# Short convolution's blocks in pairs by seven products ahead of linear attention, other filler in their place, and the down stages' h kept in float32

## The chip, the cores and the metric

One core of a Trainium2 chip runs the whole program in one launch. The metric is the device time of that launch in microseconds, the median of the runs. The engines are TensorE (PE: matrix products and transposes), VectorE (DVE), ScalarE (ACT), GpSimd (POOL) and SyncE (SP, which issues most transfers). Each works through its own instructions in the order in which they stand in the program, and waits at one until what it needs is there.

## The reference

One layer of an encoder is applied to two groups of tokens with the same weights: x_sample with 512 tokens (stream S in the kernel) and x_prompt with 256 (stream P), 1024 features each, in float32.

```python
x = LN(a*x + 0.5*swiglu(x, ffn1_gu, ffn1_down))        # 2816 hidden
x = LN(a*x + parallel_mixer(x))
x = LN(a*x + memory_cross_attention(x, mem, ...))      # 256 memory rows, 4 heads of 256
x = LN(a*x + 0.5*swiglu(x, ffn2_gu, ffn2_down))

# parallel_mixer: one projection x @ w_in gives all of these
h, gb, gc, q, k, v, g, lr_f, lr_b, m_conv, m_gla = split(x @ w_in)
y_conv = (gb * short_conv(gc * h, conv_w)) @ w_conv_out     # width 512, three taps along the tokens
o      = gla_forward(q, k, v, lr_f) + gla_backward(...)     # 4 heads, chunks of 64 tokens
y_gla  = (rms(o) * norm_g * silu(g)) @ w_gla_out
merged = (sigmoid(m_conv) * y_conv + sigmoid(m_gla) * y_gla) @ w_out
```

Linear attention runs over chunks of 64 tokens: within a chunk products of q and k decayed by a running sum of log gates, between chunks a state of 64 x 128 per head and direction.

## The kernel before

**Products.** A float32 operand is split into a rounded part (fp32r, high) and the rest (low): `split` (L86) copies on ACT to the high part and subtracts on DVE for the low one. A product is then three matmuls, high x high, low x high, high x low (`mm3`, L105 to L108; tile names xh, xl for tokens and wh, wl for weights). `load_w` (L90) loads a block of weights of 128 x 1024, 512 KB, and splits it; of the loaded block (raw) there are three buffers, of the split ones five.

**Seven products.** `seven` (L410) computes two blocks of 128 output columns over all 768 tokens as a 2 x 2 product by seven products instead of eight; tokens come in halves of 384. `products(b)` (L489) issues P1, P5, P6, P3, P7, P2, P4, each 12 matmuls with 384 columns (lines L473, tiles px, py, pz); `snap` copies a sum to SBUF on ACT and `added` adds on DVE. The sums of weights that a pair needs are made by `weights_of` while the pair before runs (`behind`).

**Feed-forward.** `front1` and `front2` do the first blocks (`plain_block`, L593), then `block` (L540) takes the rest of the 22 blocks by seven products. `gated` (L560) splits every block's h into hq and stores the pair of halves in `hspill` (768 KB, or 384), and stores sums of h in `sspill`. `down_seven` (L221) multiplies h with the down weights, again by seven products (tiles dn): it loads split h as ao from `hspill` (`direct`) or float32 sums as sr from `sspill`, which it splits (`summed`); four ao buffers, three sr buffers. `down_last` does the blocks that stay in SBUF.

**Mixer.** `mixer` (L666) makes values, queries, keys and low-rank gates, then ten pairs by seven products: two for silu(g) (stored in `silud`) and eight for the two merge gates (stored in `sigd`). Then comes linear attention, head by head: `gate(h)` (L817) multiplies the low-rank gates (z on PE) and works on DVE and ACT through la, the scans c, dd, f, kin, qin, qst; `inner` (L863) transposes kin (kt), multiplies kin and qin (at), and keys with values (kv), and carries the state st on DVE; `outputs` (L911) makes o. DVE and ACT need long for that, so PE gets other work between: `fill(ns)` (L198) takes units from the generator at the head of `pending` until their stated durations reach ns. Here that is `conv()` (L945): twelve blocks of 128 output columns (h, gc and gb of the four column blocks), each for both streams; u = gc * h and the three taps follow on DVE, and `uc` stays in SBUF. How much is filled is set by GFILL:

```python
        pending.append(conv())
        g = gate(0)
        fill(GFILL[0])
        for h in range(4):
            st = inner(h, *g)
            nxt = gate(h + 1) if h < 3 else None
            fill(GFILL[1])
            outputs(h, g[3], st)
            if h % 2:
                rms_scale(h // 2)
            fill(GFILL[2])
        drain()
```

`rms_scale` (L927) squares o on ACT, sums on DVE and takes a reciprocal root in thirteen small steps; the scaling of o (acc by rms, L1008) and the output projections follow (`branch`, L1010: tiles pt, results t and sig).

**Cross attention.** `tok_out` (L1046) makes the mixer's last product and adds; after the norm `to_T` (L183) transposes the tokens (lt) into xh, xl. Stream S and stream P each have a `Cross`: `keys_values` (L1097) is a generator with eight units for keys K and eight for values V. Those of S fill around the transposes (FILL[0], FILL[1]; `drain` takes the rest ahead of `attend`, L1186), those of P likewise in P's own stage.

**Order.** The text above is program order. A layer that records the program moves instructions ahead of others that it predicts to wait, on each engine; the places quoted below are from the order that comes of it.

Of the kernel before, what the change touches and what calls it, by code (L numbers as in the profile page):

```python
# [15 lines left out]
NK = 8  # L16
# [10 lines left out]
LO_K = (5, 7)  # L27
LO_V = (1, 3)
# [4 lines left out]
GFILL = (16000, 10000, 8000)  # L33
FILL = (14000, 14000, 8000, 14000)
# [24 lines left out]
def _encoder(ctx, tc, nc, io, out, dbg):  # L59
# [161 lines left out]
    def down_seven(n, wdn, pairs, keep, dr, sd, order6, load_acc, ahead):  # L221
# [3 lines left out]
        with tc.tile_pool(name=f"seven{n}", bufs=1, reuse_waits="tile") as pool:  # L225
            V = nc.vector
            nd = len(pairs)
            raw = [pool.tile([128, 1024], F32, name=nid("raw7")) for _ in range(2)]
# [11 lines left out]
            def loaded(q, d):  # L240
                turn[0] += 1
                if turn[0] % 5 in (4, 0):
                    r = raw[turn[0] % 5 // 4]
# [11 lines left out]
            def ring():  # L255
                return pool.tile([128, 2, 2, HT], F32R, tag="ao", bufs=4, name=nid("ao"))

            def direct(t, par, d):

                if d == 0:  # L260
                    return [keep[2 * kp + par][:, t] for kp in pairs[d]]
                a = ring()
                kp = pairs[d][0]
                last_load[0] = nc.sync.dma_start(a[:].bitcast(F32), dr[:, t, par, kp:kp + 2])
                return [a[:, k] for k in range(2)]

            def summed(s, d):
                r = pool.tile([128, 2, HT], F32, tag="sr", bufs=3, name=nid("sr"))
                kp = pairs[d][0]
                last_load[0] = nc.sync.dma_start(r[:], sd[:, s, kp:kp + 2])  # L270
# [44 lines left out]
            for d in own[:-1]:  # L315
                P1(d)
                if d == 0:
                    load_acc(0, 0)
                P2(d)
            P2(own[-1])  # L320
# [89 lines left out]
    def seven(X, pool, more, tt, snap_t, sum_t):  # L410
# [78 lines left out]
        def products(b):  # L489
# [4 lines left out]
            p1 = snap(x, "p1")  # L494
            y = psum(nid("py"))[:, :HT]
# [16 lines left out]
    def ffn_fast(n, i, front, order6, src, groups, last):  # L512

        wgu, wdn = io[f"ffn{n}_gu"], io[f"ffn{n}_dn"]
        dr = dp.tile([128, 2, 2, NFB // 2, 2, HT], F32, name=f"hspill{n}")
        sd = dp.tile([128, 4, NFB // 2, HT], F32, name=f"sspill{n}")
# [21 lines left out]
        keep = {}  # L538

        def block(j, b):  # L540
            g1, x, up1, up2 = products(b)
# [18 lines left out]
        def gated(j, h32):  # L560
# [32 lines left out]
        def plain_block(j, b, before=None):  # L593
# [15 lines left out]
            gated(j, h32)  # L609
# [46 lines left out]
        down_seven(n, wdn, groups, keep, dr, sd, order6, load_acc, ahead)  # L656
# [6 lines left out]
        right.close()  # L663


    def mixer(i):  # L666
# [7 lines left out]
        mo = ExitStack()  # L674
# [20 lines left out]
        def low_rank(s):  # L695
# [7 lines left out]
            t = fx.tile([128, TT], F32, tag="big", bufs=3, name=nid("lrt"))[:32, :s.T]  # L703
# [54 lines left out]
        def big(nm):  # L758
            return fx.tile([128, TT], F32, tag="big", bufs=3, name=nid(nm))

        for k in range(4):
            a = []
            for q in (k, k + 4):
                x = big("x0")
                nc.vector.tensor_tensor(x[:], xh["all"][:, q, :].bitcast(F32), xl["all"][:, q, :].bitcast(F32),
# [7 lines left out]
        pairs = [(w_g(2 * c), w_g(2 * c + 1), AF.Silu, silud, 2 * c) for c in range(2)]  # L773
        pairs += [(wm[16 + 2 * c], wm[17 + 2 * c], AF.Sigmoid, sigd, 2 * c) for c in range(8)]
# [3 lines left out]
        for n, (_, _, fn, dst, c) in enumerate(pairs):  # L778
            g1, x, u1, u2 = products(ws)
            first, second = big("first"), big("second")  # L780
            for half, (g, u) in enumerate(((g1, u1), (x, u2))):
                hc = slice(half * HT, (half + 1) * HT)
                nc.scalar.activation(first[:, hc], g, fn)
                nc.scalar.activation(second[:, hc], u, fn, scale=-1.0)
            nc.scalar.dma_start(dst[:, c, :], first[:])
            nc.scalar.dma_start(dst[:, c + 1, :], second[:])
# [6 lines left out]
        mop = mo.enter_context(tc.tile_pool(name="mixo", bufs=1, reuse_waits="tile", side="right"))  # L793
# [14 lines left out]
        cw = gp.tile([128, 4, 3], F32, name="cw")  # L808
        nc.sync.dma_start(cw[:], io["conv_w"])
# [129 lines left out]


        uc = []
        co = {"S": slice(0, TS), "P": slice(TS + 1, TT + 1)}
        uo = {"S": slice(1, TS + 1), "P": slice(TS + 2, TT + 2)}

        def conv():  # L945
            for b in range(4):
                u = gp.tile([128, TT + 3], F32, tag="u", bufs=1, name=nid("u"))
                for z in (0, TS + 1, TT + 2):
                    nc.gpsimd.memset(u[:, z:z + 1], 0.0)
                w = load_w(wm[4 + b])  # L950
                for s in STREAMS:
                    ps = proj_T(w, s)
                    nc.scalar.activation(u[:, uo[s.name]], ps, AF.Copy)
                    yield s.T * 10.2
                w = load_w(wm[8 + b])
                for s in STREAMS:
                    ps = proj_T(w, s)
# [483 lines left out]
```

## Time and profile before

| | us |
|---|---|
| median of three runs | 1776.19 (1775.16 to 1776.35) |
| the profiled execution: its time | 1774.76 |
| its span, first to last instruction | 1773.0 |
| PE without work in the span | 17.6 |
| linear attention, first gate product to last output (724.8 to 861.4) | 136.6 |
| all DMA | 267.26 MB, mean 151 GB/s |

The profile's page gives for each engine its busy time and share of the span, for each line the groups of instructions that cost most, and the chain of work that ended last, followed back from the last instruction. Other views list what an engine waited for, one stretch in order of time, and busy time by stretches. Times in them are microseconds from the start of the span, mean durations nanoseconds. A matmul's busy time overlaps that of the next one; what a matmul costs is read from the chain, where starts follow each other.

### The profile page before, as it was taken

To read this page: it belongs to the slowest core of one execution; us is meant where nothing else is said; L and a number is where in the kernel's file an instruction comes from. 1 tells how busy PE (TensorE), PEld (TensorE's weight loads), DVE (VectorE), ACT (ScalarE), POOL (GpSimd) and SP (SyncE) were. 2 spreads that over 40 slices of the span, in tenths; PEclk is the share of its full clock that TensorE was granted. 3 is DMA by queue.
4 is the path that set the end of the run, shared out by engine and by line. 5 is a ranking of instruction groups with operands and counts; after the bars stand their busy time and mean duration, and the time that the engine had idled before them with its cause. 6 is when DMAs were issued, how large, how long until landed. Compare 5 with 4: busy or idle time off the path is not lost.

```text
span 1773.0 us, 25183 instructions
## 1 busy us (share of the span) xinstructions
PE 1755.4 (99%) x9758; PEld 1613.7 (91%) x9758; DVE 1258.9 (71%) x2157; ACT 767.1 (43%) x1297; POOL 26.0 (1%) x60
## 2 busy tenths in 40 slices
PE   9999999999999999999999999999999999999998
PEld 9999999878889999888888988899899999997886
DVE  8777777487569555579775964596697777765956
ACT  6444444243235544655232253344354444443521
POOL 0000000000100000000000000000000000000002
PEclk9999999999999999999999999999999999999999
DMA  5434333598433333311363262255424444328961
GB/s 199 152 125 156 128 137 114 195 324 300 170 108 95 125 125 125 118 36 53 122 220 131 83 191 72 84 197 162 152 85 147 139 144 140 132 88 319 346 220 72
DMA packets 100535, 267.26 MB, mean 151 GB/s; under 512 B 10016, under 2 KB 23584, under 8 KB 100416
## 3 DMA queue, kind: packets, MB, share of 16 engines
q1 hardware_dynamic: 92352, 248.88, 40.9%
q10 hardware_dynamic: 8064, 16.78, 2.6%
q8 instruction: 76, 1.25, 0.3%
q14 instruction: 43, 0.35, 0.1%
HBM read 212.15 MB, written 53.48 MB: 150 GB/s over the span
## 4 chain that ended last, share of the span: by engine, by line
PE 94%; DVE 3%; DMA 1%; ACT 1%; issue 0%; SPq 0%; DVEq 0%; ACTq 0%
PE px L473 23%; PE py L473 11%; PE dn L283 11%; PE pz L473 6%; PE pt L106 6%; PE pt L107 6%; PE pt L108 6%; PE to L108 2%; PE to L106 2%; PE to L107 2%; PE dn L107 2%; PE dn L106 2%; PE dn L108 2%; PE pp L473 1%; PE lt L191 1%; DMA raw<-in_ffn_dn_dram 1%
## 5 line engine op out<-in xcount | busy, mean ns | idle before, releaser
L88 DVE TENSOR_TENSOR wl<-raw,wh 128x512 fp32r<-128x512 f32 (+2 forms) x309 | 289.4, 939 | 167.9 <-ACT wh L87 167.2
L87 ACT ACTIVATE wh<-raw 128x512 fp32r<-128x512 f32 (+2 forms) x309 | 255.9, 831 | 333.8 <-PE pt L107 83.5
L283 PE MATMUL dn<-wh,ao 128*128 128x512 f32 x600 | 185.8, 390 | 1.7 <-DMA ao<-hspill 1.2
L106 PE MATMUL pt<-xh,wh 128*128 128x512 f32 (+2 forms) x512 | 173.1, 338 | 0.0
L107 PE MATMUL pt<-xl,wh 128*128 128x512 f32 (+2 forms) x512 | 172.4, 337 | 0.0
L108 PE MATMUL pt<-xh,wl 128*128 128x512 f32 (+2 forms) x512 | 172.0, 336 | 0.0
L283 PEld LDWEIGHTS dn<-wh,ao 128*128 128x128 f32 x600 | 112.5, 188 | 25.8 <-DMA ao<-hspill 1.6
L87 ACT ACTIVATE wh<-tt 128x512 fp32r<-128x512 f32 x156 | 95.3, 625 | 78.4 <-PE px L473 36.7
L283 PE MATMUL dn<-wl,ao 128*128 128x512 f32 x300 | 117.4, 391 | 3.1 <-DVE wl L88 3.0
L88 DVE TENSOR_TENSOR wl<-tt,wh 128x512 fp32r<-128x512 f32 x156 | 105.3, 687 | 1.9 <-ACT wh L87 0.2
L106 PEld LDWEIGHTS pt<-xh,wh 128*128 128x128 f32 x512 | 97.0, 190 | 9.8 <-issue 0.5
L108 PEld LDWEIGHTS pt<-xh,wl 128*128 128x128 f32 x512 | 96.9, 189 | 9.0
L107 PEld LDWEIGHTS pt<-xl,wh 128*128 128x128 f32 x512 | 97.0, 190 | 8.7 <-issue 0.2
L473 PE MATMUL px<-xh,wl 128*128 128x384 f32 x232 | 77.5, 334 | 0.0
L473 PE MATMUL px<-xh,wh 128*128 128x384 f32 x232 | 77.5, 334 | 0.0
L473 PE MATMUL px<-xl,wh 128*128 128x384 f32 x232 | 77.5, 334 | 0.0
L546 DVE SCALAR_TENSOR_TENSOR h<-sil,sum 128x384 f32<-128x384 f32 x78 | 43.4, 557 | 46.4 <-ACT sil L545 46.4
L545 ACT ACTIVATE sil<-sum 128x384 f32<-128x384 f32 x39 | 20.5, 525 | 118.8 <-DVE sum L485 118.8
L283 PEld LDWEIGHTS dn<-wl,ao 128*128 128x128 f32 x300 | 56.3, 188 | 17.0 <-DVE wl L88 5.5
L106 PE MATMUL dn<-wh,hr 128*128 128x512 f32 (+1 forms) x150 | 57.7, 385 | 0.0
L107 PE MATMUL dn<-wl,hr 128*128 128x512 f32 (+1 forms) x150 | 57.5, 383 | 0.0
L108 PE MATMUL dn<-wh,hr 128*128 128x512 f32 (+1 forms) x150 | 57.4, 383 | 0.0
(372 smaller groups left out, 4678.9 us busy)
## 6 DMA issues: line engine op xcount, KB each, us to landing
raw<-in_ffn_gu_dram SPq DMA_DIRECT2D x84, 512.0 KB, 3.5
raw<-in_ffn_dn_dram SPq DMA_DIRECT2D x64, 512.0 KB, 5.7
hspill<-hq SPq DMA_DIRECT2D x24, 768.0 KB, 3.7
raw<-in_w_mix_dram SPq DMA_DIRECT2D x32, 512.0 KB, 3.5
ao<-hspill SPq DMA_DIRECT2D x18, 768.0 KB, 5.8
sr<-sspill SPq DMA_DIRECT2D x32, 384.0 KB, 5.3
sspill<-hs SPq DMA_DIRECT2D x56, 192.0 KB, 2.3
hr<-hspill SPq DMA_DIRECT2D x24, 384.0 KB, 6.8
```

Of the source, the lines that this page charges most:

```text
L87: nc.scalar.activation(hi, src, AF.Copy)
L88: (lo_eng or nc.vector).tensor_tensor(lo, src, hi.bitcast(F32), op=ALU.subtract)
L106: nc.tensor.matmul(o, lh, rh, start=start, stop=False)
L107: nc.tensor.matmul(o, lh, rl, start=False, stop=False)
L108: nc.tensor.matmul(o, ll, rh, start=False, stop=stop)
L191: nc.tensor.transpose(ps[:, j * 128:(j + 1) * 128], A[:, c:c + 128], ident[:])
L283: nc.tensor.matmul(ps[t][:], l, r[:, o], start=start and k == 0 and m == 0, stop=stop and k == 1 and m == 2, skip_group_check=True)
L473: nc.tensor.matmul(ps, l[:, c], r[:, k, :], start=st and n == 0, stop=sp_ and n == 2, skip_group_check=True)
L545: nc.scalar.activation(sil[:], g, AF.Silu)
L546: ins = nc.vector.scalar_tensor_tensor(h32[:, half * HT:(half + 1) * HT], sil[:], -0.5, u, ALU.mult, ALU.mult)
```

## The change

**Convolution by pairs.** The generator conv() goes. Six pairs are added to the ten of the mixer: four with h and gc of one column block (finish u and the taps, result stored in the DRAM tile `ucd`), two with gb of two column blocks (load ucd, multiply, store). After linear attention `branch` loads ucd and splits it into xh, xl.

**Other filler.** In its place linear attention is filled with the keys of both memories (16 units) and half the values of S (4 units). The memories are loaded and split ahead of it; finished blocks go to DRAM tiles `kvdS`, `kvdP` on ACT's queue (`kept`), and `fetch` and `take` bring them back in cross attention. GFILL and FILL get smaller numbers; S drains its four remaining value units between its transposes, and P's transposes move into S's `attend`.

**h in float32.** Where a block's h isn't kept in SBUF, `gated` stores it whole (`hwhole`) and does not split it; `down_seven` loads it like the sums and splits it. The first accumulator's load stands later, sr and ao tiles are allocated at the start, the turns of the raw buffers shift. One plain block of each feed-forward has its `gated` deferred behind the first product of the next block.

```diff
-LO_K = (5, 7)
-LO_V = (1, 3)
-GFILL = (16000, 10000, 8000)
-FILL = (14000, 14000, 8000, 14000)
+GFILL = (14000, 6500, 5000)
+FILL = (8000, 14000)
...
             def direct(t, par, d):
...
-                a = ring()
                 kp = pairs[d][0]
-                last_load[0] = nc.sync.dma_start(a[:].bitcast(F32), dr[:, t, par, kp:kp + 2])
-                return [a[:, k] for k in range(2)]
+                return loaded_h(hd[:, t, par, kp:kp + 2])
...
+            def loaded_h(src):
+                r = sr.pop(0) if sr else pool.tile([128, 2, HT], F32, tag="sr", bufs=3, name=nid("sr"))
+                last_load[0] = nc.sync.dma_start(r[:], src)
                 a = ring()
                 split(a[:, :, 0, :], a[:, :, 1, :], r[:])
...
-            q = hq_tile(hs)
-            split(q[:, :, 0, :], q[:, :, 1, :], h3[:, :hs, :])
-            keep[j] = q
-            if j < NFB - 4:
-                nc.sync.dma_start(dr[:, :hs, par, kp], q.bitcast(F32))
+            if kp in last or j >= NFB - 4:
+                q = hq_tile(hs)
+                split(q[:, :, 0, :], q[:, :, 1, :], h3[:, :hs, :])
+                keep[j] = q
+                if kp in last:
+                    nc.sync.dma_start(dr[:, :, par, kp], q.bitcast(F32))
+            else:
+                nc.sync.dma_start(hd[:, :hs, par, kp], h3[:, :hs, :])
...
+        def short_conv(b):
+            def finish(g1, x, u1, u2):
+                u, c = big("u"), big("c")
...
+                for o, p, m, c0, n in ((1, g1, u1, 0, HT), (1 + HT, x, u2, 0, TS - HT), (TS + 2, x, u2, TS - HT, TP)):
+                    V.scalar_tensor_tensor(u[:, o:o + n], m[:, c0:c0 + n], -1.0, p[:, c0:c0 + n], ALU.mult, ALU.mult)
+                c1 = c[:, :TT + 1]
+                nc.scalar.activation(c1, u[:, 1:TT + 2], AF.Copy, scale=cw[:, b, 1:2])
+                V.scalar_tensor_tensor(c1, u[:, 0:TT + 1], cw[:, b, 0:1], c1, ALU.mult, ALU.add)
+                V.scalar_tensor_tensor(c1, u[:, 2:TT + 3], cw[:, b, 2:3], c1, ALU.mult, ALU.add)
+                nc.sync.dma_start(ucd[:, b, :TS], c[:, :TS])
+                nc.sync.dma_start(ucd[:, b, TS:], c[:, TS + 1:TT + 1])
+            return finish
...
+        con = [(wm[4 + b], wm[8 + b], short_conv(b)) for b in range(4)]
+        cgt = [(wm[12 + 2 * i], wm[13 + 2 * i], conv_gates(i)) for i in range(2)]
+        pairs += sig[:2] + con[:2] + sig[2:3] + cgt[:1] + con[2:] + sig[3:4] + cgt[1:] + sig[4:]
...
-        pending.append(conv())
+        def kept(s, i, ps):
+            t = gp.tile([128, 512], F32, tag="kv", bufs=3, name=nid("kvt"))
+            nc.scalar.activation(t[:], ps[:], AF.Copy)
+            nc.scalar.dma_start(kvd[s.name][:, i, :], t[:])
+
+        for s in STREAMS:
+            pending.append(mem_keys(*mems[s.name], lambda i, ps, s=s: kept(s, i, ps)))
+        pending.append(mem_values(*mems["S"], (0,), lambda i, ps: kept(S, i, ps)))
...
-            for s in STREAMS:
-                split(xh[s.name][:, b, :], xl[s.name][:, b, :], uc[b][:, co[s.name]])
+            split(*ucs[b], gate_of(ucd, b)[:])
...
         to_T(S, 1)
-        fill(FILL[0])
+        drain()
         to_T(S, 2)
         to_T(S, 3)
-        fill(FILL[1])
-        to_T(P, 0)
-        to_T(P, 1)
-        drain()
-        xs.attend()
+        xs.attend({0: [lambda: to_T(P, 0)], 1: [lambda: to_T(P, 1)]})
```

How this moves instructions is seen at three places. The first is DVE's work between the gate products of the fourth head (z, on PE) and its scaled key kin, which PE's transposes kt wait for; wl are low halves of weights for products that come later. Before, from la's last step on:

```order
L829 TENSOR_TENSOR la_7666<-la_7666,ab_7665 128x768
L88 TENSOR_TENSOR wl_8161<-raw_8159,wh_8160 128x1024
L831 SCALAR_TENSOR_TENSOR c_7678<-mask_6727,la_7666 64x768
L832 SCALAR_TENSOR_TENSOR c_7678<-mask_6727,la_7666 64x768
L842 TENSOR_TENSOR dd_7681<-c_7678 64x768 x2
L845 TENSOR_TENSOR f_7682<-dd_7681,c_7678 64x11 x2
L88 TENSOR_TENSOR wl_8227<-raw_8225,wh_8226 128x1024
L853 TENSOR_TENSOR kin_7692<-kin_7692,c_7678 128x768
```

After the change, where acc by rms is the scaling of the first two heads' o:

```order
L1065 TENSOR_TENSOR acc<-acc,rms_8346 128x6x256
L911 TENSOR_TENSOR la_8501<-la_8501,ab_8500 128x768
L86 TENSOR_TENSOR wl_8871<-raw_8869,wh_8870 128x1024
L913 SCALAR_TENSOR_TENSOR c_8513<-mask_7575,la_8501 64x768
L914 SCALAR_TENSOR_TENSOR c_8513<-mask_7575,la_8501 64x768
L924 TENSOR_TENSOR dd_8516<-c_8513 64x768 x2
L927 TENSOR_TENSOR f_8517<-dd_8516,c_8513 64x11
L86 TENSOR_TENSOR wl_8937<-raw_8935,wh_8936 128x1024
L927 TENSOR_TENSOR f_8517<-dd_8516,c_8513 64x11
L86 TENSOR_TENSOR wl_9003<-raw_9001,wh_9002 128x1024
L86 TENSOR_TENSOR wl_9139<-raw_9137,wh_9138 128x1024
L935 TENSOR_TENSOR kin_8527<-kin_8527,c_8513 128x768
```

Four low halves stand ahead of kin where there were two, and the scaling of the first two heads came between la's steps.

The second place is DVE's work after the last head's state st, ahead of the convolution's output projection (pt, t). Before, the low half xl of its operand uc stood first and the sums ms of the rms after it:

```order
L968 TENSOR_TENSOR uc_7871<-uc_7871,pt_7979 128x256
L88 TENSOR_TENSOR xl<-uc_6904,xh 128x256
L88 TENSOR_TENSOR xl<-uc_7218,xh 128x256
L88 TENSOR_TENSOR xl<-uc_7557,xh 128x256
L88 TENSOR_TENSOR xl<-uc_7871,xh 128x256
L88 TENSOR_TENSOR wl_8429<-raw_8427,wh_8428 128x1024
L933 TENSOR_REDUCE ms_8027<-sq_8028 128x6
L933 TENSOR_REDUCE ms_8027<-sq_8031 128x6
```

After the change it comes from the loaded tile sig and stands behind the whole reciprocal root and the scaling:

```order
L141 SCALAR_TENSOR_TENSOR rqt_8748<-rqt_8748,rqa_8745 128x12
L142 SCALAR_TENSOR_TENSOR rqy_8747<-rqt_8748,rqy_8747 128x12
L1019 COPY rms_8744<-rqy_8747 128x12
L1065 TENSOR_TENSOR acc<-acc,rms_8744 128x6x256
L86 TENSOR_TENSOR xl<-sig_8785,xh 128x768
L86 TENSOR_TENSOR xl<-sig_8789,xh 128x768
L86 TENSOR_TENSOR xl<-sig_8793,xh 128x768
L86 TENSOR_TENSOR xl<-sig_8797,xh 128x768
L1078 TENSOR_TENSOR t_8769<-sig_8809,pt_8811 128x512
L1078 TENSOR_TENSOR t_8769<-sig_8809,pt_8825 128x256
```

The split moved behind some fourteen steps that need the last o.

The third is PE in stream S's cross attention, from the last products ahead of the second pair of transposes lt on; K, V are products of the memory, pt those of the query. Before:

```order
L108 MATMUL K_9448<-mh_8768,wl_9481 128x256
L191 MATMUL lt_9509<-ident,acc 128x128 x4
L191 MATMUL lt_9516<-ident,acc 128x128 x4
L191 MATMUL lt_9523<-ident,acc 128x128 x4
L191 MATMUL lt_9530<-ident,acc 128x128 x4
L106 MATMUL K_9541<-mh_8756,wh_9543 128x256
L107 MATMUL K_9541<-ml_8757,wh_9543 128x256
L108 MATMUL K_9541<-mh_8756,wl_9544 128x256
```

After:

```order
L106 MATMUL V_10040<-wh_10096,ml_9478 128x512
L189 MATMUL lt_10121<-ident,acc 128x128 x4
L189 MATMUL lt_10128<-ident,acc 128x128 x4
L189 MATMUL lt_10135<-ident,acc 128x128 x4
L189 MATMUL lt_10142<-ident,acc 128x128 x4
L104 MATMUL pt_10155<-xh,wh_10150 128x512
L104 MATMUL pt_10194<-xh,wh_10189 128x512
L104 MATMUL pt_10229<-xh,wh_10224 128x512
L105 MATMUL pt_10155<-xl,wh_10150 128x512
L106 MATMUL pt_10155<-xh,wl_10151 128x512
L104 MATMUL pt_10155<-xh,wh_10150 128x512
```

Behind the transposes stood key products, which don't need them; now the query's products stand there, which multiply what was transposed, with three of high halves pulled ahead of the first low one.

More of the change, by code (lines that the diff above doesn't have):

```diff
@@ L219, in down, with down_seven @@
             tok_mm(ps, w, kk, hh[s.name, t, j], hl[s.name, t, j], first and kk == 0, stop and kk == 1, cols)
-    def down_seven(n, wdn, pairs, keep, dr, sd, order6, load_acc, ahead):
+    def down_seven(n, wdn, pairs, keep, hd, sd, order6, load_acc, ahead):
         with tc.tile_pool(name=f"seven{n}", bufs=1, reuse_waits="tile") as pool:
@@ L241, in loaded @@
                 turn[0] += 1
-                if turn[0] % 5 in (4, 0):
-                    r = raw[turn[0] % 5 // 4]
+                if turn[0] > 1 and turn[0] % 5 < 2:
+                    r = raw[turn[0] % 5]
                 else:
@@ L494, in products @@
             p1 = snap(x, "p1")
+            with tc.issue_after(marks["act"]):
+                while hooks:
+                    hooks.pop()()
             y = psum(nid("py"))[:, :HT]
@@ L536, in weights @@
             return weights_of(wgu[j], wgu[NFB + j])
-        keep = {}
+        keep, deferred = {}, []
         def block(j, b):
-            g1, x, up1, up2 = products(b)
+            g1, x, up1, up2 = products(b, deferred)
             h32 = fp.tile([128, TT], F32, tag="h32", bufs=2, name=nid("h32"))
@@ L608, in plain_block @@
             marks["dve"] = ins.ins
-            gated(j, h32)
+            if defer:
+                deferred.append(lambda: gated(j, h32))
+            else:
+                gated(j, h32)
         nx, ws = front(locals())
@@ L655, in ffn_fast @@
             ahead = lambda: load_h(js, lp, "hr", 6)
-        down_seven(n, wdn, groups, keep, dr, sd, order6, load_acc, ahead)
+        down_seven(n, wdn, groups, keep, hd, sd, order6, load_acc, ahead)
         with tc.tile_pool(name=f"down{n}", bufs=1, reuse_waits="tile") as f2:
@@ L771, in w_g, with gates @@
             return io["w_g"].rearrange("a p (b c) -> p a b c", b=2)[:, :, :, c * 128:(c + 1) * 128]
-        pairs = [(w_g(2 * c), w_g(2 * c + 1), AF.Silu, silud, 2 * c) for c in range(2)]
-        pairs += [(wm[16 + 2 * c], wm[17 + 2 * c], AF.Sigmoid, sigd, 2 * c) for c in range(8)]
+        cw = g1p.tile([128, 4, 3], F32, name="cw")
+        nc.sync.dma_start(cw[:], io["conv_w"])
+        ucd = dp.tile([128, 4, TT], F32, name="ucd")
+        V = nc.vector
+        def gates(fn, dst, c):
+            def finish(g1, x, u1, u2):
+                first, second = big("first"), big("second")
+                for half, (g, u) in enumerate(((g1, u1), (x, u2))):
+                    hc = slice(half * HT, (half + 1) * HT)
+                    nc.scalar.activation(first[:, hc], g, fn)
+                    nc.scalar.activation(second[:, hc], u, fn, scale=-1.0)
+                nc.scalar.dma_start(dst[:, c, :], first[:, :TT])
+                nc.scalar.dma_start(dst[:, c + 1, :], second[:, :TT])
+            return finish
@@ L777, in mixer @@
         marks["dve"] = last_sum
[L778 to L786, printed above, removed]
+        for n, (_, _, finish) in enumerate(pairs):
+            finish(*products(ws))
             if n + 1 < len(pairs):
@@ L791, in mixer @@
         values(range(3, 6))
-        mop = mo.enter_context(tc.tile_pool(name="mixo", bufs=1, reuse_waits="tile", side="right"))
+        mems = {}
+        for s, c0 in ((S, 0), (P, 256)):
+            mc = slice(c0, c0 + 256)
+            for c in range(4):
+                raw = wp.tile([128, 1024], F32, tag="raw", bufs=3, name=nid("mraw"))[:, :512]
+                nc.sync.dma_start(raw, io[f"mem{s.name}"][c])
+                split(xh["all"][:, 2 * c:2 * c + 2, mc], xl["all"][:, 2 * c:2 * c + 2, mc],
+                      raw.rearrange("p (a b) -> p a b", b=256))
+            mems[s.name] = tuple([x["all"][:, k, mc] for k in range(NK)] for x in (xh, xl))
         gp = gl.enter_context(tc.tile_pool(name="gla", bufs=1, reuse_waits="tile"))
@@ L1191, in attend @@
                 self.scores(h)
+                for f in others.get(h, ()):
+                    f()
+                self.take(h + 1 if h < 3 else -1, *((4, 5) if h == 0 else ()))
                 if h < 3:
```

154 lines of the change are left out of this document (78 added, 76 removed).

## The prediction

> **What bounds the kernel now.** The first view is the page's busy table with its chain of work that ended last.
>
> ```profile
> PE 1755.4 (99%) x9758; PEld 1613.7 (91%) x9758; DVE 1258.9 (71%) x2157; ACT 767.1 (43%) x1297; POOL 26.0 (1%) x60
> PE 94%; DVE 3%; DMA 1%; ACT 1%; issue 0%; SPq 0%; DVEq 0%; ACTq 0%
> ```
>
> TensorE is busy 1755.4 of 1773.0 us and carries 94% of the chain. So matmul time taken away shortens the kernel, but only if nothing makes TensorE wait instead: it idles 17.6 us in all, and there is hardly anything else to gain. The second view, the waits of PE, says where (each row: us in total, times, longest).
>
> ```profile
> PE dn L283 <- DVE wl L88: 3.0, 3, 1.3
> PE dn L283 <- DMA ao<-hspill: 1.2, 1, 1.2
> PE px L473 <- ACT snap L478: 1.2, 1, 1.2
> PE o L922 <- DVE st L907: 1.1, 1, 1.1
> PE dn L283 <- ACT wh L87: 0.5, 1, 0.5
> ```
>
> Three places have waits: the first blocks of the feed-forward stage (1.2), the starts of the two down stages (3.0 + 1.2 + 0.5 = 4.7), and the end of linear attention (1.1). In linear attention itself PE hardly waits, and the third view, busy time by windows, says why: the columns after the window are its length, then PE, PEld, DVE, ACT.
>
> ```profile
> core 0: us, PE busy (x) PEld busy (x) DVE busy (x) ACT busy (x) POOL busy (x), PEclk, DMA share, GB/s
> 724.80:861.40 136.60, 135.54 (x914) 116.74 (x912) 108.65 (x180) 75.02 (x118) 2.12 (x17) 1.00 0.16 50
> ```
>
> From the first gate product to the last output DVE has 108.65 us of work, a chain of small steps per head, and PE 135.54 us, most of it convolution blocks that fill the time in which the chain runs. This margin is what the change spends.
>
> **The change part by part.** *Matmul time.* Prices come from the chain of waits, whose rows are start, duration, what.
>
> ```profile
> 50.06 2.08 PE px L473 x12
> 779.86 0.23 PE pt L107
> 1002.26 0.12 PE K L106
> ```
>
> Removed: twelve convolution blocks, each 24 matmuls with 512 and 24 with 256 columns, 288 of each: 288 x 0.227 + 288 x 0.120 (the third row's shape) = 99.8 us; the rounded 0.23 is 0.227 by the starts of neighbouring rows. Added: six pairs by seven products of 2.08 us, 87.4 us. PE saves **12.5 us**. Keys and values of the memory are moved, not added.
>
> *Feed-forward and down stages.* 24 stores of the split h of 768 KB become stores of the whole h (384 or 192 KB), 18 loads of 768 KB become 384 KB with a split in SBUF (one copy on ACT, one subtraction on DVE, some 0.9 each), and 24 of 44 splits in the gated blocks go. The first h load of a down stage no longer waits for the last split, and the accumulators load later, so I take all the waits of the second view at these places as gone: **5.9 us** (bounds 0 and 7.1, with the issue time beside them).
>
> ```profile
> 346.35 1.07 ACT wh L87
> ...
> 348.72 18.67 PE dn L283 x81
> ```
>
> The added splits cost nothing where they stand beside PE: by the second row a matmul there takes 230 ns, so a product of twelve 2.8 us, and a split holds ACT and DVE for 0.9 each. Without that cover they would cost 18 x 0.9 = 16 us over the two stages.
>
> *Linear attention.* This is the main term. Filler falls from 99.8 us to 16 key units of 24 x 0.120 = 2.88 and 4 value units of 12 x 0.227 = 2.72, 57.0 us: PE has 135.5 - 99.8 + 57.0 = 92.7 us of work in the window. DVE loses the convolution's operations and gains eleven low halves of weights, since each unit of 2.8 us needs one where a convolution block of 8.2 us needed one too.
>
> ```profile
> L88 DVE TENSOR_TENSOR wl<-raw,wh 128x1024 fp32r<-128x1024 f32 x12 | 14.7, 1221 | 1.4 <-ACT wh L87 1.3
> L963 DVE SCALAR_TENSOR_TENSOR uc<-u,cw,uc 128x769 f32<-128x769 f32 x4 | 4.1, 1020 | 0.3
> L968 DVE TENSOR_TENSOR uc<-uc,pt 128x512 f32<-128x512 f32 x4 | 2.7, 686 | 1.4 <-PE pt L108 1.2
> L968 DVE TENSOR_TENSOR uc<-uc,pt 128x256 f32<-128x256 f32 x3 | 1.2, 414 | 0.0
> L88 DVE TENSOR_TENSOR xl<-uc,xh 128x512 fp32r<-128x512 f32 x4 | 2.7, 686 | 0.0
> ```
>
> For each of four column blocks two steps like the second row, two like the third and two like the fourth, 2 x 1.02 + 2 x 0.69 + 2 x 0.41: 17.0 in all; with xl 19.7 less; 11 x 1.22 = 13.4 more: 102.4 us. **DVE now has more to do there than PE**, so at least 9.7 us are lost; the order of its rows says how much more. One head in the timeline (start, duration, what), and its ends on PE in the chain:
>
> ```profile
> 788.64 6.03 DVE L907 SCALAR_TENSOR_TENSOR st<-st,f,kv 64x128 f32<-64x128 f32 x16 [2.45 <-ACT st L905]
> 796.96 1.22 DVE L88 TENSOR_TENSOR wl<-raw,wh 128x1024 fp32r<-128x1024 f32 x1
> 805.17 0.95 DVE L853 TENSOR_TENSOR kin<-kin,c 128x768 f32<-128x768 f32 x1
> 813.02 1.76 DVE L1008 TENSOR_TENSOR acc<-acc,rms 128x1536 f32<-128x1536 f32 x1
> ```
>
> ```profile
> 786.88 0.55 PE z L824 x2
> 798.86 0.37 PE o L922 x4
> 803.16 0.43 PE pt L106
> 817.21 0.65 PE kt L870 x6
> ```
>
> From z at 786.88 DVE works without a pause until kin at 806.12, 19.2 us later; PE comes to kt only after 30.3 us, so 11 us are spare. z (0.55) and the previous head's o (4.3) stay; of filler the second, third and fourth heads now have 5 x 2.88, 5 x 2.88 and 4 x 2.72 there, covers of 19.25, 19.25 and 15.7 us. The chain gets longer in the order, where ACT copies a finished key block in the time of this row:
>
> ```profile
> 864.33 0.60 ACT L924 ACTIVATE acc<-o 128x512 f32<-128x512 f32 x1 [0.59 <-PE o L922]
> ```
>
> - second head: two more low halves (2.44), one convolution step less (0.41), a copy of finished keys on ACT ahead of its exponentials, 0.6: 21.8, **2.6** over the cover;
> - third: one low half more and both reductions of the first two heads (0.95 each by a row below), and some 1.1 of ACT's copy and squares, an estimate; again 0.41 less: 23.0, **3.8**;
> - fourth: two more low halves, the 1.76 of acc times rms and ACT's 0.6, 0.41 less: 23.6, **7.9**.
>
> The first head's place, with the row of z from the chain as its start and the step from the timeline behind which the fifth filler unit's weights now stand:
>
> ```profile
> 724.98 0.35 PE z L824 x2
> ```
>
> ```profile
> 738.46 0.17 DVE L845 TENSOR_TENSOR f<-dd,c 64x11 f32<-64x11 f32 x1
> ```
>
> Its fifth key unit needs a low half that stands behind f: 13.5 us after z, plus a second high half on ACT (1.07 by the row of wh) ahead of the exponentials, plus 0.17 + 1.22: 15.9; PE has four units and z until 11.9: **4.0** (3.0 without the high half). Last, the fourth head's own output, which in before has filler too:
>
> ```profile
> 855.26 1.34 PE kv L899 x22
> 860.96 0.36 DVE st L907
> 861.46 0.44 PE o L922 x4
> 865.26 0.43 PE pt L107
> ```
>
> The state needs until 861.3, the last kv product ends at 856.6; with nothing but two diagonal blocks (0.4) between, PE waits some 4.4 us where it waited 1.4 with the issue time: **3.0**. In all linear attention loses 21.3 us and lasts 114.0, in which DVE is busy for 90%, against 80% before.
>
> *Convolution's output projection.* In before its operand was in SBUF. Now it is loaded after the last o (its buffer is that of the products before), and the order puts its low half on DVE behind the rms of the last two heads.
>
> ```profile
> 866.99 0.95 DVE L933 TENSOR_REDUCE ms<-sq 128x6 f32<-128x768 f32 x1 [0.20 <-ACT sq L932]
> 870.66 1.76 DVE L1008 TENSOR_TENSOR acc<-acc,rms 128x1536 f32<-128x1536 f32 x1
> ```
>
> These come 1.7 and 5.4 us after the end of o at 865.26. The scaling ends 7.2 us after o, the low half of 768 columns, 0.95 like the reduction over as many, more: **8.1 us** of wait, where before had none; 5.3 if the load alone set it: 3.5 to land, as a block of mixing weights does (the last number of the row), and some 0.9 for each half.
>
> ```profile
> raw<-in_w_mix_dram SPq DMA_DIRECT2D x32, 512.0 KB, 3.5
> ```
>
> *Cross attention of stream S.* Before put key products behind the second pair of transposes; now the query follows them directly. Its xl of four tiles stands on DVE behind two low halves of values, two steps of a norm and between small ones, eight steps of some 0.7 us like the 512-column rows above, with ACT's high half ahead of the first: 6.9 us after the transposes begin. These take 1.75, and three matmuls hoisted past the wait 0.7: **4.4** (1.0 if the norm's steps come earlier).
>
> *At nothing.* The spills of keys, values and u, and their loads, move 384 KB or less each while DMA is used to 0.16 by the window's row; the deferred splits of the plain blocks, the splits of the memory and stream P's transposes inside attention stand beside products. If one landed late, its place would wait for one landing, 3.5. The loads for the projection are the exception: on SP they wait for the last o, and the gates' loads are queued behind them, but needed later.
>
> *Pauses.* How fast PE is after a pause of 8 us no row shows. The nearest are the start and, as warm comparison, 16 matmuls of the same shape (first row a window's length, PE busy and count; the second from the chain):
>
> ```profile
> 2.30:5.74 3.44, 3.44 (x16) 3.44 (x17) 0.90 (x2) 1.26 (x4) 0.00 (x0) 1.00 0.94 275
> ```
>
> ```profile
> 1000.51 1.75 PE lt L191 x16
> ```
>
> So a cold start costs 1.7 us, while the granted clock reads 1.00 there, and the waits of at most 1.3 us cost nothing visible. I charge the two longest new waits, 7.9 and 8.1, with it: **3.4** (bounds 0, and six waits above 3.4 us: 10.2). The Trainium skill, page "TensorE: Matmul & The Clock Gate", Part 1, states that PE's clock is halved after an idle window of about 3.4 us and comes back after as long a stretch of work. By that rule all six waits above it pay, and the time is that of the third rival below.
>
> *Sum.* 21.3 + 8.1 + 4.4 + 3.4 = 37.2 lost, 12.5 + 5.9 = 18.4 won: +18.8. The profiled execution took 1774.76 (span 1773.0 and 1.76 around it): 1793.6. The median of the runs, 1776.19, stands 1.4 above it, so the forecast is **1795 us**.
>
> **The rivals.**
> 1. *DVE's idle time takes the new low halves, so the kernel gets faster.* DVE idles 136.6 - 108.65 = 28.0 us of the window. If the eleven halves fall into it, the chains keep their 19.2 us: no wait in the second and third head, 3.5 in the fourth, 3.0 in the first and 3.0 at o; the load alone sets the projection (5.3), and stream S waits for nothing: 14.8 against 12.5 + 7.1, or -4.8: 1771 by the median. It decides at the point where less than 16 us of the 34 are left. Against it: DVE works its rows in order, and those of a chain have no gap in the timeline but 2.45 for ACT.
> 2. *It doesn't do what it says: the six pairs are no faster than the blocks.* A convolution pair adds five steps on DVE, some 3.6 us, and a spill through memory. If they set the pace, the 12.5 us don't appear: 1807.
>
> ```profile
> 640.00:700.00 60.00, 60.00 (x348) 60.00 (x348) 33.59 (x53) 29.61 (x57) 0.00 (x0) 1.00 0.36 123
> ```
>
>    Against it: in 60 us of pairs of the same kind PE has no gap and DVE is busy for 33.6, or 56%; with 3.6 of a pair's 14.6 more it is some 80%.
> 3. *Every longer wait leaves PE slow.* Six times 1.7 instead of two: +6.8, 1802. For it speaks the start, against it that the clock column shows nothing.
>
> **How the numbers follow.** Forecast 0.63, first rival 0.13, second 0.10, third 0.14. A measurement of this kernel tells some 0.2% (3.5 us) from no change. Of the first rival's cases two thirds are faster by more, and a few waits more leave the time unchanged, as does the lower end of the forecast, where the 9.7 of DVE's work, 7 at the projection and 1 in stream S are all: faster 0.09, same 0.08, slower 0.83. Range: from 1774, a little below that lower end (17.7 lost against 18.4 won), to 1808, which takes in the second and the third rival.
>
> **What would show it.** Right: in the waits of PE, K or V products and kt behind DVE (wl, kin) with about 18 us, o behind st 4, the first pt of the output projection behind xl 8, the query behind xl 4; no dn wait for ao. DVE at 90% between the first z and the last o, a window of 114 us. Six pairs of 14.6 us without gaps. Wrong: a window under 105 us (first rival), pairs above 15 us (second), matmuls after a wait at double the time for 3 us in six places (third); or waits in the down stages that stay.

## The result and the profile after

The changed kernel takes 1802.03 us (median of four runs, 1801.05 to 1804.13) against 1775.94 us before on the same chip: a ratio of 1.0148, 95% interval 1.0132 to 1.0164, or 26.1 us slower. The forecast was 1795 in a range of 1774 to 1808. The profiled execution has a span of 1800.6 us. Its page, busy times, the clock granted to PE in 40 slices, and the chain by engine:

```profile
PE 1762.7 (98%) x9686; PEld 1631.3 (91%) x9686; DVE 1298.6 (72%) x2231; ACT 787.4 (44%) x1345; POOL 25.9 (1%) x60
PEclk9999999999999999999879999999999999999999
PE 91%; DVE 6%; ACT 1%; issue 1%; DMA 1%; POOL 0%; SPq 0%; DVEq 0%; POOLq 0%; ACTq 0%
```

PE has 72 matmuls less, yet is busy for 7.3 us more, and idles 37.9 us instead of 17.6. The second row says where to look: one place with a lower clock, half way through. The waits of PE (total, times, longest):

```profile
PE kt L952 <- DVE kin L935: 8.1, 3, 5.9
PE pt L104 <- ACT xh L85: 4.6, 2, 4.1
PE pt L105 <- DVE xl L86: 4.5, 2, 2.6
PE o L1004 <- DVE st L989: 4.1, 1, 4.1
PE K L106 <- DVE wl L86: 4.1, 1, 4.1
PE warm L73 <- POOL ident masks.py:199: 2.3, 1, 2.3
PE at L961 <- DVE qin L937: 1.5, 2, 1.2
PE sc L106 <- DVE ql L86: 0.8, 1, 0.8
```

The waits of the down stages are gone, and those forecast are there, each at its place (the row of warm is the start of the kernel, which the kernel before has too). Busy time by windows, linear attention and then the convolution's output projection (length, PE, PEld, DVE, ACT and POOL busy, the clock, and DMA's share and GB/s):

```profile
809.10:937.46 128.36, 110.50 (x801) 97.72 (x799) 105.64 (x170) 81.75 (x122) 1.60 (x8) 0.86 0.39 127
937.46:980.60 43.14, 36.45 (x194) 31.55 (x195) 21.28 (x38) 7.86 (x10) 0.00 (x0) 0.86 0.55 174
```

The mean clock is 0.86 in both. In steps of 5 us one sees it fall behind a pause and come back. The first pause is the 4.1 us in front of K, up to 825.6; then come 1.6 us up to 859.2, 0.7 and 1.2 up to 889.9, and from 911.7 on the long ones, one soon after the other:

```profile
855.00:860.00 5.00, 3.42 (x28) 3.04 (x27) 4.68 (x7) 3.96 (x7) 0.00 (x0) 1.00 0.41 112
860.00:865.00 5.00, 4.70 (x32) 4.63 (x33) 4.96 (x7) 2.38 (x5) 0.00 (x0) 0.60 0.73 243
865.00:870.00 5.00, 5.00 (x41) 4.68 (x39) 2.54 (x8) 4.88 (x11) 0.00 (x0) 0.72 0.38 119
...
890.00:895.00 5.00, 5.00 (x45) 5.00 (x47) 4.86 (x15) 2.27 (x4) 0.00 (x0) 0.67 0.78 258
...
915.00:920.00 5.00, 2.46 (x10) 2.15 (x11) 4.23 (x5) 2.27 (x4) 0.00 (x0) 0.56 0.95 331
920.00:925.00 5.00, 5.00 (x36) 5.00 (x37) 2.34 (x4) 0.00 (x0) 0.00 (x0) 0.50 0.11 36
925.00:930.00 5.00, 1.79 (x17) 1.48 (x13) 3.45 (x10) 1.08 (x4) 0.00 (x0) 0.84 0.00 0
...
940.00:945.00 5.00, 1.01 (x2) 0.50 (x2) 4.58 (x14) 3.37 (x4) 0.00 (x0) 0.50 0.62 244
...
950.00:955.00 5.00, 5.00 (x31) 4.43 (x30) 1.79 (x3) 0.00 (x0) 0.00 (x0) 1.00 0.44 146
```

What that does to the same 21 products is seen in the chain, first before and then after the change:

```profile
783.01 2.20 PE at L879 x21
```

```profile
860.37 3.65 PE at L961 x21
```

So two losses stand side by side: waits, and matmuls at half the clock behind them. Stage by stage against before: feed-forward and first down stage -5.8 us; the mixer's pairs 235.8 against 145.8, +90.0; linear attention from the first z to the last o 128.4 against 140.5, with 42.8 us of matmul time taken out of it, so 30.7 lost; the projection 43.1 against 33.5.

### The profile page after: what moved, and what is told of

It is laid out like the page before. It is cut to its first block, busy times and chain, and to the rows that moved or that the text cites. A ratio compares the mean times of both kernels' runs of the same rounds, so it can differ in the third digit from the quotient of the medians.

```text
span 1800.6 us, 25309 instructions
## 1 busy us (share of the span) xinstructions
PE 1762.7 (98%) x9686; PEld 1631.3 (91%) x9686; DVE 1298.6 (72%) x2231; ACT 787.4 (44%) x1345; POOL 25.9 (1%) x60
## 4 chain that ended last, share of the span: by engine, by line
PE 91%; DVE 6%; ACT 1%; issue 1%; DMA 1%; POOL 0%; SPq 0%; DVEq 0%; POOLq 0%; ACTq 0%
PE px L473 25%; PE py L473 13%; PE dn L284 13%; PE pz L473 6%; PE pt L105 4%; PE pt L106 4%; PE pt L104 4%; PE pp L473 3%; PE to L106 2%; PE to L104 2%; PE to L105 2%; PE dn L104 2%; PE dn L106 2%; PE dn L105 2%; DVE st L989 1%; DVE wl L86 1%
## 5 line engine op out<-in xcount | busy, mean ns | idle before, releaser
L104 PE MATMUL pt<-xh,wh 128*128 128x256 f32 (+2 forms) x320 | 109.6, 344 | 4.6 <-ACT xh L85 4.6
L105 PE MATMUL pt<-xl,wh 128*128 128x256 f32 (+2 forms) x320 | 109.2, 342 | 4.5 <-DVE xl L86 4.5
L106 PE MATMUL pt<-xh,wl 128*128 128x256 f32 (+2 forms) x320 | 108.7, 340 | 0.0
L473 PE MATMUL px<-xh,wl 128*128 128x384 f32 x280 | 93.5, 334 | 0.0
L85 ACT ACTIVATE ao<-sr 128x768 fp32r<-128x768 f32 x50 | 41.9, 844 | 70.1 <-issue 24.2
L104 PEld LDWEIGHTS pt<-xh,wh 128*128 128x128 f32 x320 | 61.5, 193 | 10.6 <-ACT xh L85 5.2
L105 PEld LDWEIGHTS pt<-xl,wh 128*128 128x128 f32 x320 | 61.5, 193 | 10.5 <-DVE xl L86 5.4
L106 PEld LDWEIGHTS pt<-xh,wl 128*128 128x128 f32 x320 | 61.6, 192 | 5.3
L478 ACT ACTIVATE snap<-px 128x384 f32<-128x384 f32 x78 | 37.8, 485 | 51.6 <-PE px L473 51.0
L104 PE MATMUL dn<-wh,hr 128*128 128x512 f32 (+1 forms) x150 | 57.7, 385 | 0.0
```

The source lines that it names most:

```text
L85: nc.scalar.activation(hi, src, AF.Copy)
L104: nc.tensor.matmul(o, lh, rh, start=start, stop=False)
L105: nc.tensor.matmul(o, lh, rl, start=False, stop=False)
L106: nc.tensor.matmul(o, ll, rh, start=False, stop=stop)
L473: nc.tensor.matmul(ps, l[:, c], r[:, k, :], start=st and n == 0, stop=sp_ and n == 2, skip_group_check=True)
L478: ins = nc.scalar.activation(t, ps, AF.Copy)
```

## The experiments

Times are medians; "before" is the kernel before in the same set of runs (1775.5 to 1776.3).

| run | us | ratio to before, 95% interval |
|---|---|---|
| the change | 1802.0 | 1.0148 (1.0132 to 1.0164) |
| e1_warm | 1808.0 | 1.0188 (1.0171 to 1.0205) |
| e2_align | 1798.7 | 1.0132 (1.0117 to 1.0147) |
| e3_down | 1766.7 | 0.9951 (0.9936 to 0.9965) |
| e4_nolow | 1795.0 | 1.0110 (1.0095 to 1.0125) |
| e5_warm2 | 1790.7 | 1.0084 (1.0067 to 1.0101) |
| e6_early | 1793.2 | 1.0095 (1.0079 to 1.0110) |
| e7_more | 1797.6 | 1.0126 (1.0109 to 1.0143) |
| e8_comb | 1788.0 | 1.0065 (1.0050 to 1.0080) |
| e9_pool | 1811.8 | 1.0200 (1.0185 to 1.0216) |
| e10_mix1 | 1765.2 | 0.9936 (0.9924 to 0.9949) |
| e11_mix2 | 1768.8 | 0.9957 (0.9945 to 0.9969) |
| e12_mix2w | 1771.1 | 0.9972 (0.9963 to 0.9981) |

**Do the pauses halve the clock?** e1_warm and e5_warm2 fill them with products that nobody reads. Shown are the calls ahead of kt, with the counts of e5_warm2, about half of those of e1_warm; others stand ahead of the other waits:

```diff
+    def keep_warm(n):
+        ps = psum(nid("kw"))
+        for _ in range(n):
+            tc.keep_in_program_order(nc.tensor.matmul(ps[:, :128], ident[:], ident[:], start=True, stop=True))
...
+            keep_warm((0, 7, 3, 26)[h])
             st = inner(h, *g)
```

> The changed kernel with matmuls that nothing reads (identity by identity) ahead of each place where TensorE waits: 36 before the first head's fifth filler unit, 14, 6 and 52 before kt of the next heads, 36 before the last o, 58 before the convolution's output projection, 18 before stream S's query. Theory, pauses halve the clock: the waits are filled, not removed, so they cost what they cost, but the granted clock stays at 1.00 in linear attention and the 17 us that slow matmuls cost go: about 1785. Rival, slow matmuls come from something else that stands there (64-row products, transfers): the clock column still falls to 0.50 in the same places and the time stays at 1802 or grows by what the added matmuls don't hide.

Measured: 1808.0, but a mean clock of 0.999 over the span instead of 0.985. The count was wrong, not the idea: each product makes two records of 0.11 us, 48 us in all where the waits are 27, so that 21 us too much went in and the kernel became only 6 slower.

> As e1_warm, with half the added matmuls at each place (18; 7, 3, 26; 18; 29; 9): one identity product in float32 took 0.22 us there, not 0.11, so that the first count lasted 48 us where the waits are 26 in all. Theory, pauses halve the clock: added matmuls of 24 us lie in the waits, the granted clock stays at 1.00 and the time falls by the 17 us of slow matmuls, to about 1785. Rival, the slow matmuls cost nothing because what waits behind them would wait anyway: 1800 or more.

Measured: 1790.7, 11.3 less than the change, between the theory's 17 and the rival's nothing. The windows of linear attention and projection:

```profile
808.90:933.00 124.10, 119.07 (x977) 107.41 (x976) 108.08 (x177) 83.03 (x124) 1.59 (x8) 0.99 0.42 138
933.00:970.00 37.00, 37.00 (x224) 32.75 (x223) 18.58 (x32) 6.76 (x8) 0.00 (x0) 1.00 0.60 182
```

The clock stays up though every product of the heads is still there: the pauses do it. Filling them won 11 of some 18 us of slow matmuls. The rest had only stood in for waiting: PE, being faster, reaches the second and third head's kt earlier, and although ten of the added products (2.2 us) stand ahead of these two, PE still waits there as long as in the change:

```profile
PE kt L957 <- DVE kin L940: 2.3, 2, 1.6
```

These waits also show that the length of a pause does not decide alone. In the changed kernel 1.58 us in front of the second head's kt and 0.30 in front of at were followed by matmuls at half the clock; in e5_warm2 the same two are 1.57 and 0.34, and the clock stays:

```profile
855.00:860.00 5.00, 3.26 (x27) 2.83 (x26) 3.55 (x6) 3.36 (x7) 0.00 (x0) 1.00 0.43 131
860.00:865.00 5.00, 4.54 (x49) 4.12 (x49) 4.96 (x8) 3.95 (x7) 0.00 (x0) 1.00 0.41 136
```

What else decides is open.

**Why are the pairs longer?** A pair lasts 14.73 us in the change and 14.56 before. The chain shows products of sums (py here) at 2.12 and others at 2.08 in the changed kernel:

```profile
603.52 2.12 PE py L473 x12
...
626.74 2.08 PE pz L473 x12
```

e2_align, which widens the tile in one more place in the same way:

```diff
-            return fx.tile([128, TT + 3], F32, tag="big", bufs=3, name=nid(nm))
+            return fx.tile([128, TT + 16], F32, tag="big", bufs=3, name=nid(nm))
```

> The changed kernel with the pairs' scratch tiles widened from 771 to 784 columns, so that tiles placed behind them start at multiples of 64 bytes again, as they did before the change; nothing else. Theory, PE reads the sums mS1 to mS4 more slowly from shifted addresses: their products go from 2.12 back to 2.08 us, a pair from 14.73 to 14.56, and the kernel from 1802 to about 1799.3. Rival, the pairs are longer because of the work beside them (spills, DVE steps): 1802, products of mS1 to mS4 still at 2.12.

Measured: 1798.7, 3.4 less, and the same product in its chain:

```profile
603.24 2.08 PE py L473 x12
```

The theory holds: these products take 2% less once the scratch tile, which the change had widened from 768 to 771 columns (12 bytes for each buffer), is a multiple of 64 bytes again. In its trace the first z comes 2.5 us earlier than in the change. The other 0.9 of the 3.4 lies behind it, where this trace has less time at half the clock.

**What do the down stages bring?** e3_down is the kernel before with that part of the diff alone.

> The kernel before with the feed-forward and down part of the change alone (h in float32, deferred splits of the plain blocks, the later accumulator load, tiles allocated first); mixer and cross attention as before. Theory: only the waits at the starts of the first blocks and of the two down stages go, 5.9 us: about 1770, so that the other parts of the change cost some 32 us. Rival, the split in the down stages costs time there or the gain came from elsewhere: 1776 or more.

Measured: 1766.7, 8.8 less than before (6 to 11 by the interval; the profiled spans differ by 8.2, 6.1 of them PE's idle time and 2.1 its busy time). Of the waits only these are left:

```profile
PE warm L75 <- POOL ident masks.py:199: 2.3, 1, 2.3
PE o L934 <- DVE st L919: 1.1, 1, 1.1
PE sc L108 <- DVE ql L88: 0.3, 1, 0.3
```

So this part is faster than forecast, and the rest of the change costs 35 us.

**Is it DVE's low halves?** e4_nolow leaves out those of the key weights (`load_high` makes the high half and hands it out twice):

```diff
-                w = load_w(io["w_xk"][2 * h + b])
+                w = load_high(io["w_xk"][2 * h + b])
```

> The changed kernel without the low halves of the key weights: their products take the high half twice, so PE does the same work and DVE 16 subtractions of 1.22 us less. Theory, low halves lengthen DVE's chain: the wait for wl in the first head (4.1) and those of the second (1.9) go, those of the third and fourth, which have value weights, stay; with the slow matmuls behind the first two, 5.7, some 11 us less: about 1791. Rival, ACT's table loads and exponentials set the chain and low halves lie in DVE's gaps: 1800 to 1802, kin as late as now.

Measured: 1795.0, 7.0 less where the theory had 11. The first head's wait for wl is gone (0.8 at kt is left there) and so is the second's. But the third head's wait for kin, with value weights ahead of it, grew from 0.7 to 2.2, and the sum for kin did not fall:

```profile
PE kt L959 <- DVE kin L942: 9.2, 3, 6.3
```

The theory holds for the heads that it names; what PE wins in one head it waits for in the next, since DVE's chain runs through all of them. e9_pool makes the same low halves on GpSimd:

```diff
-                w = load_w(io["w_xk"][2 * h + b])
+                w = load_w(io["w_xk"][2 * h + b], nc.gpsimd)
```

> The changed kernel with the low halves of the key weights made on GpSimd instead of DVE; the result is unchanged. Theory, the low halves lengthen DVE's chain: as e4_nolow, 7 us less, about 1795, if GpSimd is fast enough for one per unit. Rival, GpSimd takes longer for one than a unit lasts (2.9 us), or slows DVE beside it: the wait for wl grows and the time is 1802 or more.

Measured: 1811.8, 9.8 slower than the change: the rival, by its second branch. The waits for wl fell to 2.0 us in all, but DVE slowed down. GpSimd's row over the run, two of DVE's in the first head, the same two in a head of the kernel before (in the changed kernel's first head they take the same 954 and 1754 ns), and the wait (the groups show total and mean ns):

```profile
L86 POOL TENSOR_TENSOR wl<-raw,wh 128x1024 fp32r<-128x1024 f32 x16 | 45.0, 2843 | 25.5 <-ACT wh L85 8.4 <-issue 6.3 <-DMA raw<-in_w_xk_dram 6.2
```

```profile
L924 DVE TENSOR_TENSOR dd<-c 64x768 f32<-64x768 f32 x2 | 6.0, 3007 | 0.1
L914 DVE TENSOR_TENSOR_SCAN c<-mask,la 64x768 f32<-64x768 f32 x1 | 3.8, 3786 | 0.0
```

```profile
L842 DVE TENSOR_TENSOR dd<-c 64x768 f32<-64x768 f32 x2 | 1.9, 954 | 0.1
L832 DVE TENSOR_TENSOR_SCAN c<-mask,la 64x768 f32<-64x768 f32 x1 | 1.8, 1754 | 0.0
```

```profile
PE kt L952 <- DVE kin L935: 16.4, 4, 6.8
```

Work taken off DVE came back as slower work on DVE.

**The projection.** e6_early loads the convolution's operand before the last output and splits it ahead of the rms:

```diff
...
             if h == 3:
+                uts = [gp.tile([128, TT], F32, tag="ut", bufs=4, name=nid("ut")) for b in range(4)]
+                for b in range(4):
+                    nc.sync.dma_start(uts[b][:], ucd[:, b, :])
+                with tc.issue_after(marks["st"]):
+                    for b in range(4):
+                        split(xh["all"][:, b, :], xl["all"][:, b, :], uts[b][:])
             outputs(h, g[3], st)
...
-        for b in range(4):
-            split(*ucs[b], gate_of(ucd, b)[:])
```

> The changed kernel with the convolution's operand loaded from ucd into four tiles of its own ahead of the last head's output, and its splits put behind the last step of the state st on DVE, ahead of the rms. Theory: the projection waits 6.7 us for xh and xl because the load stands behind the last o and the low half behind the rms; that goes, and of the slow stretch after it 2 us more: about 1793. Rival, the scaling of the last two heads is what the projection's later steps need and the wait moves there: 1800 to 1802, with PE waiting at ot or a later pt.

Measured: 1793.2, 8.9 less, as expected; PE no longer waits for xh or xl there; of the 4.1 us for st, 2.7 are left.

**More filler.** e7_more takes half of P's values into linear attention:

```diff
-GFILL = (14000, 6500, 5000)
-FILL = (8000, 14000)
+GFILL = (14000, 8000, 5000)
+FILL = (5000, 14000)
...
+        pending.append(mem_values(*mems["P"], (0,), lambda i, ps: kept(P, i, ps)))
```

> The changed kernel with four more units in linear attention, half of stream P's values, taken out of P's own stage, and six units for every head (GFILL 14000, 8000, 5000). Theory, the waits are cover that is short of the chain: each unit adds 2.7 us of cover and 1.22 to DVE's chain, so the wait for kin falls from 8.1 to about 2 and the slow matmuls behind it go: some 8 to 11 us less, about 1792, if P's stage does not wait with 11 us less of filler. Rival, DVE sets the pace of linear attention: the chain grows with the cover, kin waits stay, and the time is 1799 or more.

Measured: 1797.6, 4.4 less where the theory had 8 to 11. The wait for kin went, as the theory has it, but the one at the last o grew from 4.1 to 5.0, and lt and pT wait in P's stage, which had given up its filler:

```profile
PE lt L189 <- DVE acc L175: 5.1, 2, 2.7
PE o L1004 <- DVE st L989: 5.0, 1, 5.0
...
PE pT L1220 <- DVE e L1209: 1.4, 1, 1.4
```

> e2_align, e6_early and e7_more together. Theory: the parts add up, 3.4 + 9 + 10: about 1780, with the wait for wl in the first head (4) and that of the last o (4) left with their slow matmuls; still behind the kernel with the down part alone (1766.7). Rival, what one part wins shows as a wait at the next: 1788 or more.

Measured: 1788.0, where 3.4 + 8.9 + 4.4 from the single runs would give 1785.3: nearly a sum, and the rival's number. The three repairs together stay 21 us behind e3_down.

**How much filler is spare?** e10_mix1 and e11_mix2 put h and gc of one and of two column blocks into pairs on top of e3_down; gb and the other blocks stay in conv(), keys and values in cross attention. Both have the wide scratch tile of e2_align. The lines shown are of e11_mix2; e10_mix1 has 1 for 2:

```diff
+        con = [(wm[4 + b], wm[8 + b], short_conv(b)) for b in range(2)]
+        pairs += sig[:2] + con + sig[2:]
...
+                if b < 2:
+                    nc.sync.dma_start(c[:, co["S"]], ucd[:, b, :TS])
+                    nc.sync.dma_start(c[:, co["P"]], ucd[:, b, TS:])
```

> e3_down with h and gc of one column block of the convolution by a pair ahead of linear attention; gb of it and the other three blocks stay as filler (GFILL 15600, 8000, 2000), keys and values stay in cross attention. Filler falls from 99.8 to 83.2 us. Theory, filler above the chain's need of some 60 us is spare, so this much can go without a wait: one pair of 14.56 for two blocks of 8.32 each, 2.1 us less than e3_down, about 1764.6. Rival, any filler less shows as a wait with slow matmuls behind it, as in the change: 1767 or more.

Measured: 1765.2, the fastest kernel here; against e3_down 1.5 us, which the intervals do not tell from nothing, though its trace has no wait above 0.6 us but the start's.

> The same with two column blocks by pairs and no filler after the third and fourth head's o: filler 66.6 us, against 17 us needed in the first head, 14.4 in each other, and 4.4 ahead of the last o. Theory: 4.2 us less than e3_down and some 1.5 us of new waits, at the first head and the last o: about 1764. Rival, DVE's chain is the bound already: waits at kt of 2 us and more in each head and slow matmuls behind them, 1768 or more.

Measured: 1768.8. There is one wait of 1.6 at the fourth head's kt, and the 5 us windows behind it show what it drags along:

```profile
PE kt L907 <- DVE kin L890: 1.6, 1, 1.6
```

```profile
840.00:845.00 5.00, 3.53 (x29) 2.12 (x28) 4.88 (x9) 3.26 (x6) 0.00 (x0) 0.98 0.00 2
845.00:850.00 5.00, 4.83 (x25) 4.50 (x26) 5.00 (x8) 2.05 (x5) 0.00 (x0) 0.50 0.01 3
850.00:855.00 5.00, 5.00 (x36) 4.78 (x36) 4.05 (x9) 1.11 (x5) 0.00 (x0) 0.50 0.03 6
855.00:860.00 5.00, 5.00 (x40) 4.13 (x39) 4.58 (x14) 2.22 (x4) 0.00 (x0) 1.00 0.28 101
```

Ten us at half the clock behind a pause of 1.6. The second pair should have won 2.1 over e10_mix1 by its matmul time and lost 3.6 instead, 5.7 apart.

> e11_mix2 with eight identity products that nothing reads (0.22 us each, 1.8 in all) ahead of the fourth head's kt, the one place where PE waits there (1.6 us, with the clock at 0.50 for the 10 us behind it). Theory, this one pause is what halves the clock: it is filled but costs its 1.6 us as before, the clock stays at 1.00, and at, kv and the filler behind it take 4 to 5 us less: about 1764.5. Rival, the clock falls because of what follows (products of 64 rows), pause or not: 1768.8 and the clock at 0.50 in the same place.

Measured: 1771.1, neither, and no faster than e11_mix2. The windows show both halves of the answer:

```profile
845.00:850.00 5.00, 4.12 (x50) 3.76 (x49) 5.00 (x8) 1.52 (x4) 0.00 (x0) 1.00 0.00 0
...
860.00:865.00 5.00, 5.00 (x15) 3.71 (x16) 3.60 (x10) 2.28 (x4) 0.00 (x0) 0.50 0.61 167
```

```profile
PE o L964 <- DVE st L949: 2.0, 1, 2.0
```

With the pause filled the clock stays at 1.00 behind kt: the heads' 64-row products alone do not lower it, it takes the pause. But PE then comes earlier to what follows, waits 0.9 for kT and 2.0 at o for st, and the clock falls behind that. Here the time was only moved along DVE's chain.

## Why the prediction was right, and what was off

The direction, the waits behind DVE's chain and their places were right; what follows a wait on PE was not as forecast but as in the third rival, and the time came out 7 us above the forecast, at that rival's price (1802). By its own steps:

- **Matmul time, -12.5.** The pairs took 90.0 instead of 87.4; e2_align wins back 2.5 of these 2.6 us by the place of the tiles alone. The forecast took the old pairs' rate for tiles whose place the change moves.
- **Down stages, -5.9.** e3_down: -8.8 (-6 to -11). All waits went, and 2.1 us of PE's busy time, whose place stays open.
- **Linear attention, +21.3.** Waits of 4.1 for wl, 8.1 and 1.5 for kin and qin, and 3.0 more at o: 16.7. By place 4.1, 1.9, 1.9, 5.9, 3.0 against 4.0, 2.6, 3.8, 7.9, 3.0. That DVE's chain sets it is shown by e4_nolow, e7_more and e9_pool. DVE was busy for 105.6 of 128.4 us, 82%, not 90%: the slow matmuls stretched the window (in e5_warm2 it is 108.1 of 124.1, 87%).
- **Projection, +8.1.** 6.7 waited; e6_early won 8.9 with the slow matmuls behind it.
- **Stream S, +4.4.** 0.4 and 1.9 by the gaps in front of the query: 2.3.
- **Pauses, +3.4.** This is the term that was mis-sized. PE's busy time is 13.9 above its work in linear attention (110.5 against 92.7 and the 3.9 of the last o) and 2.9 in the projection, with some 1.6 in S: 18 us where the forecast had 3.4; filling the pauses won 11 of them (e5_warm2). The step failed in two ways: it charged a pause only above some length, while pauses of 1.2 to 1.6 us were followed by slow matmuls too, and it charged each once, while from the fourth head's kt on pauses follow each other so closely that the clock, by its column, was at 0.50 for some 31 of the 35 us from 915 to 950.

That the sum still came within 7 us is in part luck. Waits that were 8.1 us shorter than forecast (4.6 in linear attention, 1.4 at the projection, 2.1 in stream S) and 2.3 more won in the down stages (by the spans) made up for most of the 14.6 us by which the pauses were too cheap and the 2.6 by which the pairs were.

The first rival fell, since the low halves did lengthen the chain. The second did in part: the pairs lost a fifth of their gain, through addresses, not through DVE. The third had the mechanism; its 1.7 a pause was too little for some and its count of six too small, so its 1802 is met for the same lucky reason. What the prediction held against it was no evidence: the trace of the kernel before has no record of the clock in its first 6.3 us, and without one the column reads 1.00, so it could not show the start. The rule of the Trainium skill's page "TensorE: Matmul & The Clock Gate", Part 1, was the right one to weigh: the clock column reads 0.50 behind pauses, as it states. Its length of some 3.4 us for the pause is not what these runs show: 1.6 us were enough in e11_mix2, and the same length left the clock alone in e5_warm2.

## What to carry to other kernels

Work that covers another engine's chain cannot be cut for nothing: compare what the slower engine has to do in the stretch with what is left for PE, before counting matmuls. A wait of one or two microseconds on PE can cost several more in slow matmuls behind it, so a change that opens small waits should be priced with them, and one that closes them can win more than their length (8.9 us for 6.7 in e6_early), unless the wait only moves on, as in e12_mix2w. When a change has several parts, run each alone: here the small part was faster by 0.5% and the large one hid it.

## What the runs showed of the hardware

- A pause of 1.6 us can halve the granted clock for 10 us (e11_mix2). Two of 0.7 and 1.2 us did so for some 3.3 us (the 0.67 over 890 to 895 in the changed kernel), 1.6 and 0.3 for some 6.8 (the 0.60 and 0.72 over 860 to 870). The same 1.6 and 0.3 in e5_warm2 and the kernel before's single waits of at most 1.3 us left no mark. Length alone does not decide it; what else does, the moment at which the pause falls or the transposes kt right behind it, is open.
- A subtraction of 128 x 1024 on GpSimd takes 2.84 us (DVE 1.22), and some of DVE's steps beside it slow down, from 0.95 to 3.0 and from 1.75 to 3.8 us (e9_pool).
- A matmul with a moving operand of 384 columns took 2% longer (2.12 against 2.08 us for twelve) when three more columns in the tiles ahead shifted its address by 12 bytes each; with these tiles widened to a multiple of 64 bytes it took as long as before (e2_align).
